# Two small tiles of a hybrid decoder block get more columns, and with them the start of nearly every matmul operand moves to a multiple of 64 bytes

## The chip, the cores and the metric

One NeuronCore of a Trainium2 chip runs the whole program; the seven others are not used. The time is that of the device for one execution, in microseconds. The kernel before took 706.59 us, the median of three runs (706.48 to 708.43).

## What is computed

A decoder block on 512 tokens of width 1,024, all in float32:

```
h = rmsnorm(x, norm1_g);  proj = h @ w_in            # u, v_g, q, k, v, q_idx, k_idx, w_idx, gates
y_a = gelu(u) * (tril(w_s) @ layernorm(gelu(v_g)) + b_s)
score = sum over 8 heads of w_idx * relu(rope(q_idx) @ rope(k_idx)^T);  sel = top_k(score, 128), causal
y_b = softmax(rope(q) @ rope(k)[sel]^T / 8) @ v[sel]          # 8 heads of 64
merged = sigmoid(g0) * (y_a @ w_out_a) + sigmoid(g1) * (y_b @ w_out_b)
x = x + merged @ w_o
x = x + square(relu(rmsnorm(x) @ w_ff_in)) @ w_ff_out          # 1,024 -> 4,096 -> 1,024
return rmsnorm(x, norm_f_g)
```

## The kernel before, in words

Every product of float32 matrices is made of three matmuls: each operand is split into a rounded part (the names with h) and the rest (the names with l), and l·h, h·l and h·h are added up in PSUM. A matmul of TensorE has a *moving* operand, which streams past, and a *stationary* one, which a LDWEIGHTS (engine PEld in the rows) has put into the array before. Most matmuls here have 512 moving columns of 4 bytes.

The program goes through these stages, which follow each other on TensorE; the two-letter names are those of the rows:

- `va` (L277): values, index keys and index weights, with the tiles `wah`, `wal`, `wa` moving. Then `qi` (index queries), `vg` and `u` (`gmlp_in`, L409 to L411), with the index scores `lg` between the `vg` matmuls, then `ga` (first gates). Beside `u` and `ga` VectorE searches the 128 best scores (L509, L511).
- `k`, `q` (rotary keys and queries), `oa` (`branch_a`: the first branch's output projection).
- `gb`, the second gates, and the rest of `k` and `q`, with the heads of attention between them (`class Block`: scores `at`, L610 and L611; transposes `pt`, L629; `values`: `pv`, L641).
- `ob` (`branch_b`) and `wo` (`proj_o`), the second branch's and the block's output projection.
- `f` at L146 to L148 (`hidden`: the first matrix of the MLP) by turns with `pp` (`products`, L882 to L884: the second matrix, seven of its eight groups by a Strassen scheme with 7 products), and at the end `f` at L932 to L934 (`ff_last`: the eighth group), which also normalises and stores.

All projections that go through `gemm` (L146 to L148) have a converted weight `wh` or `wl` stationary and the activations moving. `u`, `vg` and `ff_last` have the weights moving.

The tiles come from three SBUF pools. `G` lives through the whole program: the activations `hTh`, `hTl` (later `h2h`, `h2l`), the converted weights `wh`, `wl`, and at its end some small tiles, `ssq2` (L758), `rstd2` and `fss`. `E` lies directly behind `G` and lives until L745: `VS`, the score tiles `sc`, the units `kq` and `T` (queries, keys, later `mT`), `ybt` (`yaT`, `ybs`), `pt`, and last the three buffers `p` (L242, L612). `F` takes the place of `E` for the MLP: `R2`, `raw`, `f` (the tiles `fp`), `s`, and `u` (the Strassen weights; the rows print them as `u` like the gate's `u`, with L882 to L884).

The allocator hands out space in units of 32 bytes per partition. The tiles of `G` that matmuls read start at multiples of 64 bytes. `G` ends at byte 126,048, which is 32 past a multiple of 64, so every operand in `E` and `F` starts 32 bytes past one, since all their tiles up to `p` are multiples of 64 bytes long. A buffer of `p` has 584 columns, 2,336 bytes, 36.5 times 64, so that the second of the three starts at a multiple of 64 and the two others do not. Counted over the 3,232 matmuls of the built program, by the start of the operand modulo 64:

| moving | stationary | matmuls | which |
|---|---|---|---|
| 0 | 0 | 1,749 | `qi`, `vg`, `u`, `ga`, `k`, `q`, `gb`, `f` at L146 to L148, `xn`, some of `va` |
| 32 | 32 | 784 | `pp` (588), `lg`, `sg`, `at`, `pv`, 8 that warm up |
| 32 | 0 | 536 | `wo` (192), `oa` (96), `ob` (96), most of `va` (152) |
| 0 | 32 | 157 | `f` at L932 to L934 (96), 53 transposes `pt`, 8 transposes `kti` |
| 0 | 4, 8, 12 | 6 | transposes of columns of `rstd` |

Of the kernel before, what the change touches and what calls it, by code (L numbers as in the profile page):

```python
# [10 lines left out]
F32 = mybir.dt.float32  # L11
FR = mybir.dt.float32r
# [3 lines left out]
P = 128  # L16
# [3 lines left out]
NT = S // P  # L20
# [13 lines left out]
def hybrid_block_kernel(ctx: ExitStack, tc: tile.TileContext, A: dict, out: bass.AP):  # L34
# [4 lines left out]
    G = ctx.enter_context(tc.tile_pool(name="G", bufs=1))  # L39
    ps = ctx.enter_context(tc.tile_pool(name="ps", bufs=4, space=PSUM))  # L40
    ectx = ExitStack()
    E = ectx.enter_context(tc.tile_pool(name="E", bufs=1))

    def bank(name, tag="ps"):
        return ps.tile([P, 512], F32, tag=tag, bufs=4, name=name)
# [9 lines left out]
    def unit(tag, dt, name):  # L55
        bufs = dict(kq=6, T=3)[tag]
        return E.tile([P, 2, S], dt, tag=tag, bufs=bufs, name=name)
# [162 lines left out]
    NA = 584  # L220
# [8 lines left out]
    for k in range(KD):  # L229
        if k == 0:  # L230
            h = G.tile([P, 1024], FR, tag="wh", bufs=3, name="wah0")
            l = G.tile([P, 1024], FR, tag="wl", bufs=3, name="wal0")
        elif k < 4:
            h, l = [unit("kq", FR, f"wa{c}{k}").rearrange("p a b -> p (a b)") for c in "hl"]
        elif k < 6:
            t = E.tile([P, 13, P], FR, tag="pt", bufs=2, name=f"wa{k}").rearrange("p a b -> p (a b)")
            h, l = t[:, :NA], t[:, NA:2 * NA]
        elif k == 6:
            h, l = [unit("T", FR, f"wa{c}{k}").rearrange("p a b -> p (a b)") for c in "hl"]
        else:  # L240
            h = unit("T", FR, "wah7").rearrange("p a b -> p (a b)")
            l = E.tile([P, NA], FR, tag="p", bufs=3, name="wal7")  # L242
        hl.append((h[:, :NA], l[:, :NA]))

    xn = [G.tile([P, 2, D], F32, tag="yb", bufs=2, name=f"xn{j}") for j in range(2)]
# [352 lines left out]
    class Block:  # L598
# [5 lines left out]
        def scores(self):  # L604
            h, i, N = self.h, self.i, self.N
            qs, kh, kl = kq[self.hh]
            NN = max(N, 256)
            b = bank(f"at{h}_{i}", "pa")
            q = qs[:, i * P:(i + 1) * P]
            PE.matmul(b[:, :NN], q, kl[:, :NN], start=True, stop=False)  # L610
            PE.matmul(b[:, :NN], q, kh[:, :NN], start=False, stop=True)  # L611
            self.p = p = E.tile([P, NA], F32, tag="p", bufs=3, name=f"p{h}_{i}")  # L612
            self.s3 = s3 = G.tile([P, 4], F32, tag="s3", bufs=6, name=f"s3_{h}_{i}")
            DVE.tensor_tensor_reduce(out=p[:, :N], in0=b[:, :N], in1=mb0 if i == 0 else sc[i],
                                     op0=ALU.add, op1=ALU.min, scale=-ATT_SCALE, scalar=3.0e38,
                                     accum_out=s3[:, 0:1])
            ACT.activation(p[:, :N], p[:, :N], AF.Exp, bias=s3[:, 0:1], scale=-1.0,
                           accum_out=s3[:, 1:2])
# [136 lines left out]

    acct = [half("yb", 2, f"acc{j}") for j in range(2)]
    acc = [acct[j // 2].rearrange("p (a b) c -> p a (b c)", a=2)[:, j % 2] for j in range(NT)]
    ssq2 = G.tile([P, NT], F32, name="ssq2")  # L758
    rstd2 = G.tile([P, NT], F32, name="rstd2")
    R2 = F.tile([P, S], F32, name="R2")  # L760

# [326 lines left out]
```

## Time and profile before

| | |
|---|---|
| runs, median (lowest to highest) | 706.59 us (706.48 to 708.43) |
| the profiled execution | 708.15 us |
| its span, first to last instruction | 706.4 us |
| what lies around the span | 1.75 us |
| mean granted TensorE clock | 0.996 of full speed |
| TensorE busy | 694.0 us (98%), 3,232 matmuls |
| VectorE busy | 559.5 us (79%) |
| ScalarE busy | 330.1 us (47%) |
| GpSimd busy | 55.0 us (8%) |
| DMA, mean over the span | 116 GB/s |

A matmul's duration in the rows runs from its issue to the modelled end of its output, and the next one starts long before that: the rate of a stream is read from the distance between the starts of two matmuls, which the text calls the spacing. Where the rows are given to a tenth of a microsecond, a spacing is worked out over many matmuls.

### The profile page before, as it was taken

The numbers are of one execution on the slowest core, as the hardware profiler recorded it, in microseconds if no ns is written. First come the engines' busy times: TensorE is split into PE (matmuls) and PEld (weight loads), VectorE is DVE, ScalarE is ACT, GpSimd is POOL, SyncE is SP. The second block draws the span as 40 slices with busy tenths as digits, with TensorE's granted clock in tenths as the row PEclk, the third lists the DMA queues.
The fourth block names the chain that finished last, engine by engine and source line by source line (L and its number), as shares of the span: only waits on it lengthen the run. The fifth ranks groups of instructions, "written<-read, shape, count | busy, mean of one in ns | idle before, by whom it ended". The sixth has DMA issues, their size and how long they took to land.

```text
span 706.4 us, 8948 instructions
## 1 busy us (share of the span) xinstructions
PE 694.0 (98%) x3232; PEld 576.4 (82%) x3232; DVE 559.5 (79%) x1035; ACT 330.1 (47%) x568; POOL 55.0 (8%) x41
## 2 busy tenths in 40 slices
PE   8999999899999999999999999999999999999996
PEld 8998888688888888778888888888888888888884
DVE  5678899987657877877443978979798997979995
ACT  6645633233235545563246765445352544535133
POOL 0043352420000000000000000000000000000001
PEclk9999999999999999999999999999999999999999
DMA  8735131233752463214442233142333214233023
GB/s 321 269 99 161 61 114 60 89 120 106 193 150 60 138 169 112 68 58 144 149 175 94 90 117 110 43 155 84 123 116 119 86 41 163 69 129 111 1 59 119
DMA packets 27356, 82.02 MB, mean 116 GB/s; under 512 B 4784, under 2 KB 6192, under 8 KB 25264
## 3 DMA queue, kind: packets, MB, share of 16 engines
q10 hardware_dynamic: 14688, 59.78, 26.2%
q1 hardware_dynamic: 12624, 21.67, 9.7%
q8 instruction: 25, 0.41, 0.2%
q14 instruction: 19, 0.16, 0.1%
HBM read 71.48 MB, written 2.10 MB: 104 GB/s over the span
## 4 chain that ended last, share of the span: by engine, by line
PE 86%; DVE 9%; issue 2%; ACT 1%; POOL 1%; DMA 0%; POOLq 0%; ACTq 0%
PE f L148 8%; PE f L146 8%; PE f L147 8%; PE pp L884 6%; PE pp L882 6%; PE pp L883 6%; PE va L277 4%; DVE sc L511 2%; PE wo L147 2%; PE wo L148 2%; PE wo L146 2%; DVE m L509 2%; PE gb L148 2%; PE gb L146 2%; PE gb L147 2%
## 5 line engine op out<-in xcount | busy, mean ns | idle before, releaser
L51 ACT ACTIVATE wh<-wr 128x1024 fp32r<-128x1024 f32 x88 | 92.9, 1056 | 120.1 <-PE f L148 39.6
L52 DVE TENSOR_TENSOR wl<-wr,wh 128x1024 fp32r<-128x1024 f32 x69 | 84.0, 1220 | 22.1 <-ACT wh L51 20.0
L146 PE MATMUL f<-h2h,wl 128*128 128x512 f32 x256 | 100.2, 391 | 0.0
L148 PE MATMUL f<-h2h,wh 128*128 128x512 f32 x256 | 100.0, 390 | 0.0
L147 PE MATMUL f<-h2l,wh 128*128 128x512 f32 x256 | 99.9, 390 | 0.0
L51 ACT ACTIVATE u<-w2r 128x512 fp32r<-128x512 f32 x98 | 59.2, 624 | 75.8 <-DVE w2r L810 25.4
L884 PE MATMUL pp<-u,fp 128*128 128x512 f32 x196 | 76.4, 390 | 0.0
L883 PE MATMUL pp<-u,fp 128*128 128x512 f32 x196 | 76.4, 390 | 0.0
L882 PE MATMUL pp<-u,fp 128*128 128x512 f32 x196 | 72.1, 390 | 0.0
L895 DVE TENSOR_TENSOR P<-pp,P 128x512 f32<-128x512 f32 x84 | 54.5, 683 | 18.2 <-PE pp L884 18.0
L52 DVE TENSOR_TENSOR u<-w2r,u 128x512 fp32r<-128x512 f32 x98 | 64.4, 682 | 4.3 <-ACT u L51 4.3
L148 PEld LDWEIGHTS f<-h2h,wh 128*128 128x128 f32 x256 | 48.1, 188 | 10.1
L147 PEld LDWEIGHTS f<-h2l,wh 128*128 128x128 f32 x256 | 48.1, 188 | 10.0
L146 PEld LDWEIGHTS f<-h2h,wl 128*128 128x128 f32 x256 | 48.1, 188 | 10.0
L52 POOL TENSOR_TENSOR wl<-wr,wh 128x1024 fp32r<-128x1024 f32 x19 | 46.5, 2447 | 72.2 <-ACT wh L51 52.7
L882 PEld LDWEIGHTS pp<-u,fp 128*128 128x128 f32 x196 | 36.8, 188 | 7.9
L883 PEld LDWEIGHTS pp<-u,fp 128*128 128x128 f32 x196 | 36.8, 188 | 7.8
L884 PEld LDWEIGHTS pp<-u,fp 128*128 128x128 f32 x196 | 36.8, 188 | 7.8
L51 ACT ACTIVATE fp<-fs 128x256 fp32r<-128x256 f32 (+1 forms) x28 | 17.6, 629 | 29.6 <-DVE fs L860 17.0
L838 DVE SCALAR_TENSOR_TENSOR fr<-f,R 128x512 f32<-128x512 f32 x32 | 21.9, 686 | 10.7 <-PE f L148 8.7
L146 PE MATMUL ga<-hTh,wl 128*128 128x512 f32 x64 | 25.8, 404 | 2.6 <-DVE mA L459 2.1
L965 POOL TENSOR_TENSOR fss<-fss,mhalf 128x1 f32<-128x1 f32 x4 | 2.2, 547 | 317.7 <-DVE fss L964 317.7
(251 smaller groups left out, 1556.7 us busy)
## 6 DMA issues: line engine op xcount, KB each, us to landing
wr<-in_f ACTq DMA_DIRECT2D x36, 512.0 KB, 3.5
w2r<-in_f2p ACTq DMA_DIRECT2D x14, 1024.0 KB, 4.9
wr<-in_wt ACTq DMA_DIRECT2D x26, 512.0 KB, 3.6
wr<-in_wuv ACTq DMA_DIRECT2D x8, 512.0 KB, 3.8
kq<-k_T SPq DMA_DIRECT2D x64, 64.0 KB, 2.8
wr<-in_wo ACTq DMA_DIRECT2D x8, 512.0 KB, 3.5
xT<-in_xT SPq DMA_DIRECT2D x8, 256.0 KB, 5.3
xn<-in_xn SPq DMA_DIRECT2D x2, 1024.0 KB, 8.7
```

The lines of the kernel that those rows point to most:

```text
L51: ACT.activation(hi, src, AF.Copy)
L52: (eng or DVE).tensor_tensor(lo, src, f32(hi), op=ALU.subtract)
L146: PE.matmul(dst, wl[:, k], bh, start=(k == 0), stop=False)
L147: PE.matmul(dst, wh[:, k], bl, start=False, stop=False)
L148: PE.matmul(dst, wh[:, k], bh, start=False, stop=(k == K - 1))
L277: PE.matmul(acc[j][n][:, :CUT[n].stop - CUT[n].start], a[:, j * P:(j + 1) * P], b[:, CUT[n]], start=(k == 0 and q == 0), stop=(k == KD - 1 ...
L509: DVE.max(out=m8[i], in_=sc[i])
L838: DVE.scalar_tensor_tensor(r, b, 0.0, R2, op0=ALU.max, op1=ALU.mult)
L882: PE.matmul(b[j], fl, u[:, 0], start=(q == 0), stop=False)
L883: PE.matmul(b[j], fh, u[:, 1], start=False, stop=False)
L884: PE.matmul(b[j], fh, u[:, 0], start=False, stop=(q == 1))
L895: DVE.tensor_tensor(sums[name, j], b[j], sums[name, j], op=ALU.add)
```

## The change

The buffers `p` get 592 columns in place of 584, 2,368 bytes or 37 times 64, at both places that allocate them; what is read and written of them stays the same. `ssq2` is allocated with 16 columns and used in its first four, so that `G` ends at byte 126,080, a multiple of 64. The order of the instructions, their shapes and their waits are the same on every engine.

```diff
@@ 242, the loading of the first weights
-            l = E.tile([P, NA], FR, tag="p", bufs=3, name="wal7")
+            l = E.tile([P, 592], FR, tag="p", bufs=3, name="wal7")
@@ 612, Block.scores
-            self.p = p = E.tile([P, NA], F32, tag="p", bufs=3, name=f"p{h}_{i}")
+            self.p = p = E.tile([P, 592], F32, tag="p", bufs=3, name=f"p{h}_{i}")
@@ 758, before the MLP
-    ssq2 = G.tile([P, NT], F32, name="ssq2")
+    ssq2 = G.tile([P, 16], F32, name="ssq2")[:, :NT]
```

After it 3,209 matmuls have both operands at 0 modulo 64. The others are 16 of `va`, whose tile `wal` for two of the eight input blocks starts 2,336 bytes into a `pt` buffer, and seven transposes of single columns.

## Rows read from the trace of the kernel before

**Rows 1.** The page's first part: busy time, share of the span and instructions of each engine; and the first line of its fourth part, the shares of the engines in the chain of work that ended last.

```profile
PE 694.0 (98%) x3232; PEld 576.4 (82%) x3232; DVE 559.5 (79%) x1035; ACT 330.1 (47%) x568; POOL 55.0 (8%) x41
...
PE 86%; DVE 9%; issue 2%; ACT 1%; POOL 1%; DMA 0%; POOLq 0%; ACTq 0%
```

**Rows 2.** Timeline of TensorE in the gate `u`, first and last matmul of 96 (both operands at 0). Columns: start in us, duration in us, engine, line, operation, tiles, shape, count.

```profile
80.88 0.39 PE L409 MATMUL u<-wh,hTl 128*128 128x512 f32 x1
...
102.41 0.39 PE L411 MATMUL u<-wh,hTh 128*128 128x512 f32 x1
```

**Rows 3.** Timeline of TensorE in one group of `pp`, first and last of 64 matmuls (both operands at 32); same columns.

```profile
441.88 0.39 PE L882 MATMUL pp<-u,fp 128*128 128x512 f32 x1
...
456.19 0.39 PE L882 MATMUL pp<-u,fp 128*128 128x512 f32 x1
```

**Rows 4.** Timeline of TensorE in the three long runs with one operand at 32 and the other at 0: `oa` (first, and the 91st), `wo` (first and last of 192), `f` of `ff_last` (first and last of 96); same columns.

```profile
177.39 0.40 PE L146 MATMUL oa<-yaTh,wl 128*128 128x512 f32 x1
...
198.40 0.40 PE L146 MATMUL oa<-yaTh,wl 128*128 128x512 f32 x1
...
319.42 0.40 PE L146 MATMUL wo<-mT,wl 128*128 128x512 f32 x1
...
363.98 0.40 PE L148 MATMUL wo<-mT,wh 128*128 128x512 f32 x1
...
676.86 0.39 PE L932 MATMUL f<-wh,fp 128*128 128x512 f32 x1
...
699.02 0.39 PE L934 MATMUL f<-wh,fp 128*128 128x512 f32 x1
```

**Rows 5.** `ob` by line from 303 us on: count, shortest, median and longest duration in ns, first and last start in us, shape.

```profile
L147 PE MATMUL ob<-ybsl,wh x23: 389/396/425, 303.0 to 318.9; 128*128 128x512 f32 x23
```

**Rows 6.** Timeline of TensorE where a run of `pp` (both at 32) gives way to `f` (both at 0): six starts in a row, of which the third to fifth are left out; columns as in rows 2.

```profile
419.85 0.40 PE L884 MATMUL pp<-u,fp 128*128 128x512 f32 x1
420.09 0.39 PE L146 MATMUL f<-h2h,wl 128*128 128x512 f32 x1
...
421.01 0.39 PE L147 MATMUL f<-h2l,wh 128*128 128x512 f32 x1
```

**Rows 7.** Stages: length in us, TensorE's busy time and the matmuls that overlap the stage, granted clock, DMA share, GB/s. The first is the MLP from the first Strassen group to the last `f` of `hidden`.

```profile
396.00:676.60 280.60, 280.60 (x1234) 1.00 0.29 98
```

**Rows 8.** Timeline of TensorE in the first `f` after four transposes of 128 columns, all operands at 0; between the last two rows stand six more `f`; columns as in rows 2.

```profile
368.65 0.27 PE L769 MATMUL xn<-ident,x1T 128*128 128x128 f32 x1
368.68 0.48 PE L146 MATMUL f<-h2h,wl 128*128 128x512 f32 x1
368.99 0.39 PE L147 MATMUL f<-h2l,wh 128*128 128x512 f32 x1
...
370.61 0.39 PE L148 MATMUL f<-h2h,wh 128*128 128x512 f32 x1
```

**Rows 9.** Timeline of TensorE in the heads of attention: gates `gb` (both at 0) behind the scores `at` (both at 32, 384 columns); between the last two rows stand ten more `gb`; columns as in rows 2.

```profile
207.28 0.34 PE L611 MATMUL at<-kq 128*128 128x384 f32 x1
207.46 0.40 PE L146 MATMUL gb<-hTh,wl 128*128 128x512 f32 x1
...
210.00 0.39 PE L148 MATMUL gb<-hTh,wh 128*128 128x512 f32 x1
```

**Rows 10.** `va` by line in two stretches: 11.4 to 17.6 us (all moving operands at 32), and the two input blocks whose moving tiles lie by turns at 32 and at 0; columns as in rows 5.

```profile
L277 PE MATMUL va<-wah,hTl x17: 279/309/309, 11.2 to 17.5; 128*128 128x328 f32 x9, 128*128 128x256 f32 x8
L277 PE MATMUL va<-wah,hTh x16: 277/295/313, 11.3 to 17.2; 128*128 128x256 f32 x8, 128*128 128x328 f32 x8
L277 PE MATMUL va<-wal,hTh x16: 280/295/310, 11.4 to 17.4; 128*128 128x256 f32 x8, 128*128 128x328 f32 x8
...
L277 PE MATMUL va<-wa,hTh x32: 278/296/315, 18.5 to 24.6; 128*128 128x256 f32 x16, 128*128 128x328 f32 x16
L277 PE MATMUL va<-wa,hTl x16: 276/295/319, 18.7 to 24.8; 128*128 128x256 f32 x8, 128*128 128x328 f32 x8
```

**Rows 11.** The chain of work that ended last, in order of time, around the search of the best scores: start in us, length in us, what. Behind it, of the waits, TensorE's longest.

```profile
79.86 0.62 POOL sc L446
80.50 0.69 DVE m L509
...
132.94 0.47 PE ga L146
...
PE ga L146 <- DVE mA L459: 2.1, 1, 2.1
```

**Rows 12.** VectorE late in the program: the stage from 640 to 676 us with all engines (columns: length, then TensorE, LDWEIGHTS, VectorE, ScalarE and GpSimd busy, granted clock, DMA share, GB/s), and the waits of the last additions for TensorE.

```profile
640.00:676.00 36.00, 36.00 (x160) 29.73 (x160) 34.96 (x55) 12.51 (x19) 0.00 (x0) 1.00 0.20 60
...
DVE acc L940 <- PE f L934: 2.7, 4, 0.9
```

**Rows 13.** VectorE beside `f` in 423 to 438 us: a subtraction of a Strassen weight pair in `F` (at 32) and one of a weight in `G` (at 0); then one line of `f` in the same stretch, every third of its matmuls (columns as in rows 5).

```profile
426.36 1.28 DVE L52 TENSOR_TENSOR u<-w2r,u 128x512 fp32r<-128x512 f32 x2
...
430.04 1.22 DVE L52 TENSOR_TENSOR wl<-wr,wh 128x1024 fp32r<-128x1024 f32 x1
...
L148 PE MATMUL f<-h2h,wh x22: 389/389/389, 423.3 to 437.6; 128*128 128x512 f32 x22
```

**Rows 14.** VectorE's additions of `products`, two in a row: the first pair is that of the first product, whose sums lie in `G` (at 0), the second that of the sixth, whose sums lie in `F` (at 32); columns as in rows 2.

```profile
649.90 1.28 DVE L895 TENSOR_TENSOR P<-pp,P 128x512 f32<-128x512 f32 x2
...
663.38 1.28 DVE L895 TENSOR_TENSOR P<-pp,P 128x512 f32<-128x512 f32 x2
```

## The prediction

> **What bounds the kernel now.** I read the page's busy times first, then the chain of work that ended last. TensorE is busy in 98% of the span and holds 86% of the chain [rows 1]. So outside the few places where it waits, a nanosecond taken from the distance between two matmuls is a nanosecond of the program. Nothing else is to be had here: the change alters no instruction, only where operands begin, so I ask of the trace whether the spacing of equal matmuls goes with the start of their operands.
>
> The duration in the rows does not tell it, being 0.39 to 0.40 us everywhere; the starts do. With both operands at 0 modulo 64, `u` starts 96 matmuls in 21.53 us, which over 95 distances is 226.6 ns [rows 2]. With both at 32, `pp` starts 64 in 14.31 us, or 227.1 ns [rows 3]. The same 512 columns with one operand at 32 and the other at 0 take longer: `oa` 21.01 us over 90 distances, 233.4 ns; `wo` 44.56 over 191, 233.3; `f` of `ff_last` 22.16 over 95, 233.3 [rows 4]. In the first two of these the moving operand is the one at 32, in the third the stationary one. So a start at 32 costs nothing by itself, as `pp` shows; what costs 6.6 ns, as I read it, is that the two operands of a stream differ.
>
> A changeover does it too. Where `pp` (both at 32) gives way to `f` (both at 0), the next five distances average 232 ns (1.16 us from 419.85 to 421.01) before they come down [rows 6]. I read this as the weight load of the next matmul running beside the present one, so that for a while one stream reads at 32 and the other at 0, and the pace takes some matmuls to settle.
>
> **The change part by part.**
>
> *`ssq2` wider.* It moves the whole of `E` and `F` by 32 bytes. The four mixed stages become stages with both operands at 0:
> - `wo`: 192 matmuls by 6.6 ns (233.3 less 226.7) are 1.27 us.
> - `oa`: 96 by 6.6 are 0.63 us; the last few stand among scores of other widths, so 0.6.
> - `f` of `ff_last`: 96 by 6.6 are 0.63 us.
> - `ob`: at most 0.63 us. Its last 69 matmuls run at a mean of 241 ns (15.9 us over 66 distances of the line with 23), with a wait in them [rows 5], and its first 27 stand among the heads, so I take 0.5.
>
> Together 3.0 us, all on TensorE's path. Nobody waits less or more by it: the additions behind `ff_last` wait for TensorE, 2.7 us in four waits [rows 12], and follow it.
>
> *The Strassen groups.* From 396.0 to 676.6 us `f` and `pp` fill 280.6 us with 1,234 matmuls, one of which began before [rows 7]: 227.6 ns each, 0.9 over the 226.7 of an undisturbed run. 1,233 by 0.9 are 1.1 us, which the changeovers between 0 and 32 cost. After the change there is no such changeover; I take 1.0 us.
>
> *Heads of attention.* Here `gb`, `k` and `q` (288 matmuls of 512 columns) at 0 alternate with scores and values at 32. Behind a score the next `gb` run at 230.9 ns (2.54 us over 11 distances) [rows 9]. But a change of width alone disturbs as much: behind transposes of 128 columns, with everything at 0, `f` runs at 231.4 ns (1.62 us over 7 distances from 368.99) [rows 8]. The widths stay, so I take 0.0 here. The bounds are 0 and 288 by 4.2, which is 1.2 us. The same holds for `vg` between the index scores, and what it might gain, at most 96 by 6.6 or 0.6 us, lies ahead of VectorE's search of the scores, which holds the chain from 79.9 to 132.9 us and ends in TensorE's longest wait, 2.1 us [rows 11]. It would only make that wait longer: 0.
>
> *`va`.* 152 matmuls of 256 and 328 columns have the moving operand at 32. No stretch at 0 of this shape is undisturbed, so its gain is bounded: if it paid as the wide ones do, 120 by 6.6 or 0.8 us (the 32 others keep a partner at the other residue); if not, 0. The nearest rows are of `va` itself: 49 matmuls with all moving operands at 32 take 6.3 us over 48 distances, 131 ns, while the two blocks that alternate between 32 and 0 take 6.3 over 47, 134 ns [rows 10]. What hurts there is alternation, and the two blocks keep it, with 0 and 32 exchanged. I take 0.
>
> *`p` wider.* It only moves the `p` buffers. Their transposes are issued among matmuls of other shapes; I take 0, with the heads' bound above over it. The eight more columns are never touched.
>
> *VectorE and ScalarE* read and write `E` and `F` at the new starts. Two additions into sums in `G`, at 0, and two into sums in `F`, at 32, take 1.28 us alike [rows 14], so nothing changes for them.
>
> The sum is 3.0 + 1.0 = 4.0 us. The durations are those of the profiled execution, 708.15 us with a span of 706.4, which would become 704.15 and 702.4. That execution lay 1.56 us over the median of the runs shown; against the median of 706.59 the forecast is **702.6 us**. The bounds on this reading: with heads and half of `va` gained too, 5.6 us or 701.0; with the long runs alone and part of that lost, 2.4 us or 704.2. A measurement of this kernel tells about 0.3%, 2.1 us, from no change.
>
> **The rivals.**
>
> *The residue is not the cause* (0.11). In all four slow stages one operand lies in `G` and the other in `E` or `F`; in `u`, `f` and `pp` both lie in the same region. The trace before cannot part these: it has no wide run with operands in two regions and the same residue. If the distance or the pool makes the 233.3 ns, the mixed stages keep it, and with the changeovers alike, the time stays at 706.6. For it speaks that confounding; against it, that the two blocks of `va` whose moving tiles alternate between 32 and 0 within the one region `E` are slower than their neighbours by 3 ns a matmul [rows 10].
>
> [...]
>
> *TensorE gains, VectorE keeps part of it* (0.05). VectorE works 34.96 of the 36.0 us up to 676 [rows 12]. If it, not TensorE, sets the pace of the last groups and of the combining before the last additions, the 1.0 us of the groups and the 0.6 us of `ff_last` are lost, and 2.4 us remain: 704.2. Against it: TensorE waits nowhere there (36.00 of 36.0 us busy), and the last additions wait for it.
>
> *Slower* (0.04). What counts may be the place within 64 bytes at which TensorE reads against that at which VectorE and ScalarE work in `G`. Today `pp` reads at 32 beside engines that work much at 0; afterwards all stand at 0. If `pp` then took the slow spacing, 588 by 6.6 are 3.9 us, and if the mixed stages kept theirs, the time is 710.5. It turns the sign as soon as `pp` loses more than the rest gains: with nothing gained elsewhere by any rise of its 227.1 ns, with the 3.0 us of the mixed stages by 5.1 ns. Against it: `f`, at 0, keeps 227 ns (14.3 us over 63 distances) in a stretch where VectorE writes `wl` in `G`, at 0 too [rows 13].
>
> **How the numbers follow.** The forecast has 0.80, the rivals 0.11, 0.05 and 0.04. Faster by over 0.3% are the forecast and the second rival, 0.85; within 0.3% the first, 0.11; slower 0.04. The range takes the forecast's bounds and the second rival, with 0.4 us for the median of few runs: 701.0 to 704.6. It leaves out the other two, 0.15.
>
> **What would show it.** In the profile after: `wo` over 191 distances in 43.3 us (226.7 ns) in place of 44.56; `oa` and `f` of `ff_last` likewise; no swell of five distances where `pp` meets `f`, and the stretch of the groups shorter by 1 us with the same 1,233 matmuls; `u` and long `pp` runs as before; heads and `vg` as before, within 1 us; VectorE's and ScalarE's means unchanged. The forecast is wrong if `wo` stays at 233.3 ns, and the residue then is not what slows it. It is wrong in size if the heads come down to 227 ns or if `va` moves.

## The result, and the profile after

The change made the kernel faster: 702.62 us, median of four runs (702.37 to 702.70), against 707.51 us for the kernel before beside it (706.48 to 708.92, four runs); the ratio is 0.993, 95% interval 0.9916 to 0.9944. The runs of the kernel before lie at two levels some 2 us apart (706.5 and 708.4 to 708.9), which the experiments trace to a stretch of lower clock (0.91 granted from 125 to 145 us, against 1.00) that kernels with the change's alignment show too; the four runs after all lie at the lower level, so level for level the gain here is 3.9 us (706.5 to 702.6). The forecast was 702.6 us.

The profiled execution takes 702.70 us with a span of 701.0. Of the page, the lines that answer to [rows 1]:

```profile
PE 688.8 (98%) x3232; PEld 576.1 (82%) x3232; DVE 559.0 (80%) x1035; ACT 330.0 (47%) x568; POOL 55.0 (8%) x41
...
PE 87%; DVE 9%; issue 2%; POOL 1%; ACT 0%; POOLq 0%; DVEq 0%
```

TensorE's busy time fell by 5.2 us, the span by 5.4; the other engines' busy time is the same within 0.5 us. Where it fell, the timeline of TensorE shows (start in us, duration in us, engine, line, operation, tiles, shape, count): `u`, first and last of 96; `oa`, first and 91st; `wo`, first and last of 192; `f` of `ff_last`, first and last of 96.

```profile
81.29 0.39 PE L409 MATMUL u<-wh,hTl 128*128 128x512 f32 x1
...
102.82 0.39 PE L411 MATMUL u<-wh,hTh 128*128 128x512 f32 x1
...
176.06 0.39 PE L146 MATMUL oa<-yaTh,wl 128*128 128x512 f32 x1
...
196.46 0.39 PE L146 MATMUL oa<-yaTh,wl 128*128 128x512 f32 x1
...
317.02 0.39 PE L146 MATMUL wo<-mT,wl 128*128 128x512 f32 x1
...
360.32 0.39 PE L148 MATMUL wo<-mT,wh 128*128 128x512 f32 x1
...
672.04 0.39 PE L932 MATMUL f<-wh,fp 128*128 128x512 f32 x1
...
693.58 0.39 PE L934 MATMUL f<-wh,fp 128*128 128x512 f32 x1
```

`u` keeps its 21.53 us over 95 distances, to the hundredth as in [rows 2]. The three mixed stages come down to it: `oa` 20.40 us over 90 distances, 226.7 ns; `wo` 43.30 over 191, 226.7; `f` 21.54 over 95, 226.7, where [rows 4] gave 233.3 to 233.4. Where `pp` gives way to `f`, nothing swells any more: ten distances take 2.27 us, 227 ns, against 232 in [rows 6].

```profile
416.13 0.39 PE L884 MATMUL pp<-u,fp 128*128 128x512 f32 x1
416.36 0.39 PE L146 MATMUL f<-h2h,wl 128*128 128x512 f32 x1
...
418.40 0.39 PE L146 MATMUL f<-h2h,wl 128*128 128x512 f32 x1
```

The same 1,234 matmuls of the Strassen groups now fill a stage that is 1.12 us shorter than that of [rows 7] (columns as there):

```profile
392.31:671.79 279.48, 279.48 (x1234) 1.00 0.30 98
```

The last additions wait for TensorE as in [rows 12]:

```profile
DVE acc L940 <- PE f L934: 2.2, 3, 0.8
```

Two differences of the two profiled executions are not of the change. At `va`'s end the execution after is 0.41 us later; 0.33 of it has gathered by the 57th of its 200 matmuls, a place that lies at 12.12 us before and 12.45 after, but at 12.74 and 12.09 in two other kernels with the change's alignment. (The last 0.08 us are of the change: see `va` below.) And TensorE waits for VectorE at the end of the score search in both, 2.1 us as in [rows 11]:

```profile
PE ga L146 <- DVE mA L459: 2.1, 1, 2.1
```

but in the execution before, six matmuls after it had come back, the granted clock fell for some 3.4 us (0.50 of full speed in the stage from 134.4 to 137.5 us): durations of 0.63 us, seven distances of about 427 ns. Timeline of the execution before: the sixth `ga` behind the wait, the slow stretch and the last `ga`.

```profile
134.17 0.50 PE L148 MATMUL ga<-hTh,wh 128*128 128x512 f32 x1
134.47 0.63 PE L146 MATMUL ga<-hTh,wl 128*128 128x512 f32 x1
...
136.60 0.63 PE L148 MATMUL ga<-hTh,wh 128*128 128x512 f32 x1
...
150.77 0.39 PE L148 MATMUL ga<-hTh,wh 128*128 128x512 f32 x1
```

The stage of 20 us around it (length, TensorE's busy time and matmuls, granted clock, DMA share, GB/s), before and then after:

```profile
125.00:145.00 20.00, 17.80 (x70) 0.91 0.33 105
```

```profile
125.00:145.00 20.00, 17.44 (x76) 1.00 0.34 105
```

The same two `ga` in the timeline after:

```profile
134.54 0.39 PE L148 MATMUL ga<-hTh,wh 128*128 128x512 f32 x1
...
149.50 0.39 PE L148 MATMUL ga<-hTh,wh 128*128 128x512 f32 x1
```

From the one `ga` to the other it is 16.60 us before and 14.96 after: 1.64 us that the clock gave, not the change. From the first `oa` (177.39 and 176.06) to the last `f` (699.02 and 693.58) the change alone is left: 521.63 us and 517.52, 4.11 us.

### The profile page after: what moved, and what is told of

Its sections match the earlier page's. It is cut to its first block, busy times and chain, and to the rows that moved or that the text cites. A ratio compares the mean times of both kernels' runs of the same rounds, so it can differ in the third digit from the quotient of the medians.

```text
span 701.0 us, 8948 instructions
## 1 busy us (share of the span) xinstructions
PE 688.8 (98%) x3232; PEld 576.1 (82%) x3232; DVE 559.0 (80%) x1035; ACT 330.0 (47%) x568; POOL 55.0 (8%) x41
## 4 chain that ended last, share of the span: by engine, by line
PE 87%; DVE 9%; issue 2%; POOL 1%; ACT 0%; POOLq 0%; DVEq 0%
PE f L146 8%; PE f L147 8%; PE f L148 8%; PE pp L882 6%; PE pp L883 6%; PE pp L884 6%; PE va L277 4%; DVE sc L511 2%; DVE m L509 2%; PE gb L146 2%; PE gb L147 2%; PE gb L148 2%; PE wo L147 2%; PE wo L148 2%; PE wo L146 2%
## 5 line engine op out<-in xcount | busy, mean ns | idle before, releaser
L51 ACT ACTIVATE fp<-fs 128x256 fp32r<-128x256 f32 (+1 forms) x28 | 17.6, 628 | 29.7 <-DVE fs L860 17.0
```

The source lines that it names most:

```text
L51: ACT.activation(hi, src, AF.Copy)
```

## The experiments

Two theories stood at first: **A**, that the spacing of wide matmuls goes with the difference between the starts of their two operands modulo 64, and **C**, that a start off 64 bytes costs by itself. The rows below give `wo` by line (count, shortest, median and longest duration in ns, first and last start in us): 64 starts of every third matmul are 189 distances.

**One edit at a time.** `ssq2` alone:

```diff
-    ssq2 = G.tile([P, NT], F32, name="ssq2")
+    ssq2 = G.tile([P, 16], F32, name="ssq2")[:, :NT]
```

> Only ssq2 is widened; the buffers p stay at 584 columns, so that two of the three start at 32. Theory A (the spacing goes with the difference between the two operands' starts modulo 64, and E and F move as a whole): as the full change, 702.6 us within 0.5; wo at 226.7 ns. Rival B (the wider p rows are part of the gain, through the transposes): 0.5 us or more above 702.6.

702.53 us (six runs), ratio 0.9936, interval 0.9923 to 0.995: the whole effect.

```profile
L146 PE MATMUL wo<-mT,wl x64: 389/389/389, 317.3 to 360.1; 128*128 128x512 f32 x64
```

42.8 us over 189 distances are 226.5 ns. The buffers `p` alone (L242 and L612, `NA` to 592):

> Only the buffers p are widened; E and F stay 32 bytes past a multiple of 64. Theory A: no change against the kernel before, 706.5 to 708.5 us, wo at 233.3 ns. Rival B: some of the 4 us appears, 706 us or less.

Ratio 1.0001, interval 0.999 to 1.0012, and `wo` as before, 44.1 us over 189, 233.3 ns. The wider `p` does nothing.

```profile
L146 PE MATMUL wo<-mT,wl x64: 395/396/396, 319.8 to 363.9; 128*128 128x512 f32 x64
```

**Everything at 32**, by a tile of 32 bytes ahead of all others of `G`:

```diff
+    pad = G.tile([P, 8], F32, name="pad")
+    nc.gpsimd.memset(pad, 0.0)
     hTh = [G.tile([P, S], FR, tag="hTh", bufs=KD, name=f"hTh{k}") for k in range(KD)]
```

> The full change with a 32-byte tile put first in G, so that G, E and F all start 32 bytes past a multiple of 64: 3,209 matmuls have both operands at 32. Theory A (only the difference counts): as the full change, 702.6 us within 0.7, wo and u at 226.7 ns. Rival C (a start off 64 bytes costs by itself, and pp escaped for another reason): all wide matmuls at 230 ns or more, 2,800 by 3.3 to 6.6 ns over the full change, 711 to 721 us.

Six runs, two at 702.3 and 702.6, four from 704.3 to 704.5; ratio 0.9949, interval 0.9934 to 0.9963. The upper level is the slow stretch behind the wait again (its profiled execution has a granted clock of 0.91 from 125 to 145 us). `wo` by line, which takes 42.8 us, and that stage:

```profile
L146 PE MATMUL wo<-mT,wl x64: 389/389/389, 318.7 to 361.5; 128*128 128x512 f32 x64
```

```profile
125.00:145.00 20.00, 17.44 (x69) 0.91 0.34 106
```

C falls: 3,209 matmuls off a multiple of 64 run as fast as 3,209 on one. **The mirror image**, the same `pad` and the wide `p`, but `ssq2` as before, so that `G` is at 32 and `E` and `F` at 0:

> The 32-byte tile first in G and wide p, but ssq2 as before: now G starts at 32 and E and F at 0, the mirror image of the kernel before. Theory A: as the kernel before, 706.5 to 708.5 us; wo, oa, ff_last at 233.3 ns, pp and u at 226.7, and the changeovers between pp and f are back (1,233 matmuls in 280.6 us). Rival C (the start of one operand alone counts, for instance the moving one of wo, now at 0): wo and oa at 226.7 ns and ff_last, whose moving weights are now at 32, at 233.3: about 704.5 us.

Ratio 1.0008, interval 0.9998 to 1.0019: the kernel before, with the pools' roles exchanged. `wo` and, by line, `f` of `ff_last` (32 starts, 93 distances) are at 44.1 us and 21.7 us, 233.3 ns both, and the 1,233 matmuls of the Strassen groups take 280.37 us from the first start to the last, as in the kernel before, where the change has 279.25 (behind the two added lines the numbers of lines are higher by 2):

```profile
L146 PE MATMUL wo<-mT,wl x64: 395/396/397, 318.3 to 362.4; 128*128 128x512 f32 x64
...
L934 PE MATMUL f<-wh,fp x32: 393/396/397, 675.7 to 697.4; 128*128 128x512 f32 x32
```

So the relation of the two starts counts, as A says. Whether its unit is 64 bytes, none of these can tell.

**A kernel that only streams**, 36 matmuls for each pair of starts, here condensed:

```python
for m in (0, 4, 8, 16, 32, 48, 64):            # moving operand, bytes from its tile's start
    for s in (0, 4, 8, 16, 32, 48, 64):        # stationary operand
        for r in range(36):
            PE.matmul(b, st[r % 2][:, s // 4:s // 4 + P], mv[r % 2][:, m // 4:m // 4 + 512], ...)
```

> Not the block: a kernel that only streams matmuls (its output is a copy of the last one's result). 49 blocks of 36 matmuls of 512 columns, two moving and two stationary tiles by turns, with the moving operand starting 0, 4, 8, 16, 32, 48 or 64 bytes past a multiple of 64 and the stationary one likewise; then blocks of 384, 328, 256 and 128 columns for the four pairs of 0 and 32. Theory A (the difference of the two starts modulo 64 counts): 226.7 ns on the diagonal and for 0 against 64, 233.3 for 0 and 32 either way round, and for 16 or 48 something between 226.7 and 240. Theory A2 (only the half of a 64-byte block in which a start lies counts): 0, 4, 8 and 16 are alike, and slow against 32 and 48. Theory D (any unequal pair is slow by the same 6.6 ns). For the narrower widths A expects the unequal pairs slower, by up to 6.6 ns, if the va blocks had hidden it, or no difference.

Timeline, a block a row (start, duration of the whole block): 0 with 0, 0 with 32, 0 with 64, 32 with 32, 64 with 64.

```profile
17.98 8.38 PE L40 MATMUL m0s0x<-mv,st 128*128 128x512 f32 x36
...
51.24 8.44 PE L40 MATMUL m0s32x<-mv,st 128*128 128x512 f32 x36
...
67.85 8.45 PE L40 MATMUL m0s64x<-mv,st 128*128 128x512 f32 x36
...
285.58 8.39 PE L40 MATMUL m32s32x<-mv,st 128*128 128x512 f32 x36
...
418.27 8.39 PE L40 MATMUL m64s64x<-mv,st 128*128 128x512 f32 x36
```

Less the last matmul's 0.39 us, over 35 distances: 228.3, 230.0, 230.3, 228.6 and 228.6 ns. Equal starts at 0, 32 and 64 are the quicker ones, but 0 with 64 is not among them, and 0 with 32 stays far under the 233.3 ns of the whole kernel. It missed A's figures, and A2 and D fare no better: the mean of the distances from the 12th to the 35th, from the starts in the trace, is 230.0 for 16 with 16 and 228.3 for moving 16 with stationary 4. In the built program the two moving tiles lie 2,176 bytes apart and the two stationary ones 640. So at equal starts the two operands of one matmul agree modulo 256, but each lies 128 bytes off those of the matmuls beside it; that this is what keeps equal starts at 228.3 ns is argued and not tested. By the same mean the narrower shapes respond in part: for 384 columns 173.3 ns (moving 32, stationary 0) to 176.7 (the other way round), with the equal pairs between; for 256 columns 116.7, but 120.0 with the stationary operand at 32 and the moving one at 0; for 328 columns 150.0 and for 128 columns 111.7 in all four pairs. This called for moving the pools by 64 and 128 bytes, and for a better grid.

**`E` and `F` 64 bytes further on**, every operand still at a multiple of 64:

```diff
-    ssq2 = G.tile([P, 16], F32, name="ssq2")[:, :NT]
+    ssq2 = G.tile([P, 32], F32, name="ssq2")[:, :NT]
```

> The full change with ssq2 of 32 columns in place of 16, so that E and F start another 64 bytes on: every operand is still at 0 modulo 64, but those in E and F are 64 off those in G modulo 128. Theory A (difference modulo 64): as the full change, 702.5 us within 0.5, wo at 226.7 ns. Theory A128 (the unit is 128 bytes or more; the streaming kernel had 228.3 ns for equal starts and 230.0 for 0 against 64): wo, oa and ff_last above 226.7 ns and the changeovers back, 703.5 to 706.8 us.

704.6 to 705.2 us in seven runs, 706.6 to 706.9 in five; ratio 0.9972, interval 0.996 to 0.9984. Half of the gain is gone. `wo`, which moves from `E`, takes 43.3 us over 189 distances, 229.1 ns; `f` of `ff_last`, whose stationary operand is in `F`, 21.7 over 93, 233.3. The 1,233 matmuls of the Strassen groups take 280.13 us from start to start, against 279.25 with the change, so the changeovers cost again. A misses, and A128 foretold it:

```profile
L146 PE MATMUL wo<-mT,wl x64: 392/392/394, 317.0 to 360.3; 128*128 128x512 f32 x64
...
L932 PE MATMUL f<-wh,fp x32: 393/396/398, 673.4 to 695.1; 128*128 128x512 f32 x32
```

**128 bytes further on** (48 columns):

> The same with ssq2 of 48 columns: E and F 128 bytes on, equal to G modulo 128, 128 off modulo 256. Theories A and A128: as the full change, 702.5 us. Theory A256 (the unit is 256 bytes or more): wo above 226.7 ns, 703.5 to 706.8 us.

706.3 to 707.0 and 708.2 to 708.6 us; ratio 0.9995, interval 0.9984 to 1.0007. All of the gain is gone, with 3,209 matmuls at multiples of 64 and every operand of 512 columns' matmuls at a multiple of 128, as A256 foretold. `wo` takes 44.0 us, 232.8 ns:

```profile
L146 PE MATMUL wo<-mT,wl x64: 390/393/404, 318.4 to 362.4; 128*128 128x512 f32 x64
```

A falls as it was put: 64 bytes are not the unit.

**The grid again**, with all tiles equal modulo 2,048 and the order of `gemm`, condensed too:

```python
t, c = r % 3, r // 3 % 8 * P
PE.matmul(b, st[t != 0][:, s // 4 + c:s // 4 + c + P], mv[t == 1][:, m // 4:m // 4 + 512], ...)
```

> A kernel that only streams matmuls (its output is a copy of the last one's result), now with the order of gemm: two stationary tiles by turns, moved on by 512 bytes every third matmul, and two moving ones, all tiles equal modulo 2,048. Blocks of 36 with the moving operand 0, 4, 8, 16, 32, 64, 96, 128, 256 or 512 bytes on and the stationary one 0, 16, 32, 64, 128 or 256. Theory A: 226.7 ns wherever the difference is a multiple of 64, 233.3 for 32 and 96. Theory A128: 226.7 for differences that are multiples of 128 alone. Theory A512: for 0 and 512 alone. Starts off 16 bytes (4 and 8): 233 to 237 whatever the partner, as in the first streaming kernel.

The mean of a block's distances from the 12th to the 35th, in ns, from the starts in the trace:

| moving, bytes | stationary 0 | 16 | 32 | 64 | 128 | 256 |
|---|---|---|---|---|---|---|
| 0 | 226.7 | 226.7 | 233.3 | 233.3 | 232.3 | 226.7 |
| 4 | 236.7 | 236.7 | 236.7 | 233.3 | 235.9 | 236.7 |
| 8 | 233.3 | 233.5 | 233.3 | 233.3 | 233.3 | 233.3 |
| 16 | 231.7 | 233.3 | 226.7 | 234.6 | 233.3 | 231.7 |
| 32 | 233.3 | 226.7 | 226.7 | 233.3 | 234.3 | 233.3 |
| 64 | 228.9 | 231.8 | 233.3 | 226.7 | 233.3 | 228.9 |
| 96 | 233.3 | 230.0 | 233.3 | 233.3 | 233.3 | 233.3 |
| 128 | 233.3 | 233.3 | 233.3 | 228.9 | 226.7 | 232.1 |
| 256 | 226.7 | 226.7 | 233.3 | 233.3 | 232.1 | 226.7 |
| 512 | 226.7 | 226.7 | 233.3 | 233.3 | 232.1 | 226.7 |

The timeline of some blocks, whole durations (the first and the fourth row are the two directions of 64 bytes, the first with 35 matmuls in its row):

```profile
43.49 8.33 PE L43 MATMUL m0s64x<-mv,st 128*128 128x512 f32 x35
...
118.97 8.55 PE L43 MATMUL m8s0x<-mv,st 128*128 128x512 f32 x36
...
177.71 8.55 PE L43 MATMUL m16s16x<-mv,st 128*128 128x512 f32 x36
...
269.36 8.40 PE L43 MATMUL m64s0x<-mv,st 128*128 128x512 f32 x36
...
294.34 8.32 PE L43 MATMUL m64s64x<-mv,st 128*128 128x512 f32 x36
...
369.45 8.56 PE L43 MATMUL m128s0x<-mv,st 128*128 128x512 f32 x36
...
461.00 8.33 PE L43 MATMUL m256s256x<-mv,st 128*128 128x512 f32 x36
...
469.16 8.32 PE L43 MATMUL m512s0x<-mv,st 128*128 128x512 f32 x36
```

8.32 us less 0.39 over 35 distances are 226.6 ns, 8.40 are 228.9, 8.55 are 233.1. The columns for 0 and 256 are alike to 1.2 ns, and so are the lines for 0, 256 and 512: the unit in this grid is 256 bytes. Equal places within it are quick (226.7 ns at 0, 32, 64 and 128), but for 16 with 16 (233.3); of the unequal ones 0 with 16, 16 with 32 and 32 with 16 are as quick (226.7). The direction counts: moving 64 ahead 228.9, stationary 64 ahead 233.3, the very pair that the kernel showed 64 bytes on (`wo` 229.1, `ff_last` 233.3). The difference alone does not settle it, since 96 with 32 is also 64 ahead and takes 233.3. This is theory **F**, and it made one more forecast for the whole kernel.

**256 bytes further on** (80 columns):

> The full change with ssq2 of 80 columns: E and F 256 bytes further on than with 16. Theory F (formed after the last four runs: the position of both operands within 256 bytes counts, and equal positions are fast): as the full change, 702.5 us within 0.5 in the lower of the two levels, wo at 226.7 ns. Rival (the unit is larger than 256, or the distance itself counts): 703.5 to 706.8 us.

Two runs at 702.3 and 702.5 us, four from 704.2 to 704.7; ratio 0.9943, interval 0.9929 to 0.9957; `wo` back at 42.9 us over 189, 227.0 ns, and a granted clock of 0.91 in the profiled execution, one of the upper level.

```profile
L146 PE MATMUL wo<-mT,wl x64: 389/389/389, 318.5 to 361.4; 128*128 128x512 f32 x64
```

```profile
125.00:145.00 20.00, 17.60 (x69) 0.91 0.33 105
```

**The wait behind the score search**, taken away on top of the change:

```diff
     def gate_a(m):
-        b = bank(f"ga{m}")
+        b = bank(f"ga{m}", "pa" if m % 2 else "ps")
```

> The full change, and the gates ga take their PSUM banks by turns from both sets of four, so that TensorE need not wait for VectorE's evacuation at the end of the score search. The wait (2.1 us, by the starts 2.2) goes. Theory E (the 1.7 us that separate the two levels of all these kernels are the stretch behind that wait in which the granted clock is lower in some executions): about 700.3 us, and all runs within 0.6 us of each other. Rival: the wait moves to the next consumer of VectorE's results (sg), and the level stays near 702.5 with two levels.

701.28 us (701.06 to 701.45, four runs), ratio 0.9908, interval 0.9892 to 0.9924: 1.3 us under the change, not 2.2. The wait for VectorE is gone from the list; TensorE gets on to the next converted weights sooner and now waits 1.2 us for GpSimd, where it was 0.5, and 0.8 for ScalarE, where it was 0.4. The granted clock stays at 1.00 in the stage from 125 to 145 us (second view).

```profile
PE ga L146 <- POOL wl L52: 1.2, 2, 0.7
PE kti L390 <- ACT kst L381: 0.8, 1, 0.8
```

```profile
125.00:145.00 20.00, 18.80 (x82) 1.00 0.35 104
```

**The last 16 matmuls of `va`** too:

```diff
-            h, l = t[:, :NA], t[:, NA:2 * NA]
+            h, l = t[:, :NA], t[:, 640:640 + NA]
```

> The kernel with the gates' banks from both sets, and the second half of the two pt buffers that hold first weights begins at column 640 in place of 584, so that the last 16 matmuls of va come to the common position within 256 bytes. Theory F: at most 48 matmuls by 6 ns, 0.0 to 0.3 us under 701.3. Theory E (no wait for VectorE behind the score search, so no stretch at a lower granted clock): again one level alone, all runs within 0.6 us. Rival to E: some runs 1.7 us above the others.

701.33 us (700.92 to 701.79, five runs), ratio 0.9911, interval 0.9898 to 0.9924: no difference from the kernel above can be told, and the 0.87 us between its runs are more than the 0.6 expected. Both are faster than the change. Nine runs of the two kernels without the long wait, and none at an upper level. Of four kernels with a common place that have the wait, three show both levels (`ssq2` alone at the upper one in one run of six, everything at 32 and 256 bytes further on in four of six each); the change itself shows the lower one in all four runs. All four profiled executions at an upper level have the granted clock of 0.91 behind the wait, all five at a lower level with the wait 1.00.

## Why the prediction was right, and where its reading was wrong

- **The four mixed stages**, 3.0 us: `oa` 0.61 by 90 distances, `wo` 1.26, `f` of `ff_last` 0.62. `ob` was put at 0.5 and the heads at 0; from the first `gb` to the first `wo` (200.04 to 319.42 before, 198.08 to 317.02 after) it is 0.44 for both together, but only 0.19 of it from the first `ob` to the last (24.79 to 24.60 us). So `ob` was put too high and the heads too low, by some 0.3 and 0.2: right in sum.
- **The Strassen groups**, 1.0 us: 1.12, and no distance there is over 227 ns, where the kernel before had 221 that were. Right.
- **`vg`, `p`, VectorE and ScalarE at 0**: right; `vg` takes 30.3 us in both profiles, `p` alone measured 1.0001, and VectorE is busy for 559.5 us before and 559.0 after, ScalarE for 330.1 and 330.0.
- **`va` at 0**: right in size, but not because its pace ignores the layout. Its last 144 matmuls, from the starts in the traces, take 19.00 us in all three profiles with the pools 32 bytes apart, 19.05 to 19.08 in the six with a common place, 19.12 at 64 bytes and 19.26 at 128. For these shapes of 256 and 328 columns the common place is not the quickest. In the two blocks of [rows 10] that alternate, the spacing fell from 134.3 to 133.4 ns, though they still alternate; in the two blocks ahead of them it rose from 132.2 to 133.3. Alternation by itself was not what hurt there, and [rows 10], given to a tenth, show 3 ns where the starts give 2.
- **TensorE's path**: 4.1 us of spacing gave 3.9 us of time in these runs, and 4.3 in the larger set around `ssq2` alone (706.8 to 702.5, lower levels). The last additions still wait for TensorE (2.2 us in three waits, where it was 2.7 in four), so the rival that VectorE keeps part of the gain did not occur; nor did the slower one, since `pp` stays at 226.7 ns.
- **The sum against the profiled execution** was 704.15 us and it took 702.70: the execution before held 1.64 us of the lower clock, which the prediction had not set aside, though the wait that precedes it stands in [rows 11]. Against the median it came out because the runs shown then lay, two of three, at the lower level, and so did all four runs after. That the two medians met to 0.02 us is luck.
- **The step that failed** is the reading of [rows 2 to 4], that a stream is slowed when the two starts differ modulo 64. The unit is 256: in the second grid 256 with 0 has 226.7 ns, 0 with 64 and 128 with 0 have 233.3. In the built program before, the operands of matmuls of 512 columns lay at 128 modulo 256 in `G` and at 96 in `E` and `F`, so that the pairs unequal modulo 64 were the pairs unequal modulo 256; and by luck the 16 columns of the change bring both to 128. With 32 or 48 columns the prediction would have been the same 702.6 us, and wrong: 704.9 and 706.6, the medians at the lower level.
- **The first rival** named the confounding rightly, but by the pool: `wo` at 226.5 ns across two pools excludes the pool, and 227.0 with 256 bytes more between them the distance itself. The same instruction takes 226.7 or 233.3 ns by the relation of the two starts. In the second grid a moving operand 4 bytes on has 233.3 to 236.7 ns with whatever partner, but 8 bytes on 233.3 to 233.5, which many pairs of multiples of 16 take too; the first grid had one exception, 230.0 for 4 with 16. Nor are two multiples of 16 enough: 16 with 16 has 233.3.

What makes a stream settle at one pace or the other, why 16 with 16 is slow and 0 with 16 quick, why the direction of 64 bytes matters, and why `va` is quickest 32 bytes apart, stays open. The runs show that both starts count (`wo` at 226.7 and 233.3 ns); that the cause is the weight load running beside the present matmul, as [rows 6] were read, they do not show.

## What to carry to other kernels

Where TensorE is the bound, compare the starts of equal matmuls in stages that differ in their tiles: 3% of spacing (226.7 against 233.3 ns) hides behind durations that all print as 0.39 or 0.40 us (`wo` by line has 395 to 396 ns with unequal places and 389 with equal ones). Lay out all pools that feed streams of 512 columns so that their operands stand at the same place within 256 bytes (0, 32, 64 and 128 had 226.7 ns in the second grid, 16 with 16 had 233.3); a small tile at the end of a pool shifts everything behind it. And when a trace fits a rule of alignment, shift the layout by other amounts before the rule is believed: 64 and 128 bytes fitted the words of this change, and they undid half of it and all of it.

## What the runs showed of the hardware that was not expected

- The spacing of 512-column float32 matmuls, each with a new weight load, takes values from 226.7 to 236.7 ns by the starts of the two operands within 256 bytes. Narrower shapes respond less, and otherwise: in the first grid 384 columns had 173.3 to 176.7 ns and 256 columns 116.7 to 120.0, and `va`'s 256 and 328 columns were quickest 32 bytes apart (19.00 us against 19.08 at a common place).
- After a change of width or of relation two to ten distances pass before a stream has settled (in the profile before, from the starts in the trace: two of 233 and 230 ns for `gb` behind 203.01 us, ten of 224 to 236 for `gb` from 207.46 on); one settled stream follows another of the same relation without a swell (no distance over 227 ns among the 1,233 matmuls of the Strassen groups after).
- TensorE's wait behind the score search (2.1 us in the profiles before and after) is followed in four profiled executions by a granted clock of 0.91 from 125 to 145 us (in the one before it was 0.50 for 3.4 us of them) and in five by 1.00, which goes with two levels of time 1.7 to 2.0 us apart; without the wait the two profiles have 1.00 there, and the nine runs no upper level.
